# Twelve start offsets inside the split weight tiles of a two-layer hybrid decoder

## The chip, the core and the metric

The kernel runs on one core of a Trainium2 chip. The metric is the device time of one execution in microseconds. The kernel before took 1251.52 us, the median of 2 runs that lie between 1251.26 and 1251.78 us.

## What is computed

Two decoder layers over 512 tokens of width 1024, all in float32. Cut to its skeleton:

```python
def hybrid_layer(x, p_i, positions, ...):
    h = x @ w_in                                  # 1024 -> 1704 columns: queries, keys, values, indexer
    oa = swa_sink_attention(...)                  # 8 heads, window of 128, learned sinks
    ob = dsa_sparse_attention(...)                # 8 heads, the 128 best keys of each query
    mix = concatenate([oa, ob]) @ w_o             # 1024 x 1024
    x = layer_norm(DN_ALPHA * x + mix)
    g, u = split(x @ w_gu, 2)                     # 1024 -> 2 x 2816
    ffn = (silu(g) * u) @ w_down                  # 2816 -> 1024
    ple = (p_i @ w_pp) * sigmoid(x @ w_pg)        # 256 x 1024 and 1024 x 1024
    return layer_norm(DN_ALPHA * x + ffn + ple)

def reference(x, ...):
    x = layer_norm(x)
    for i in range(2):
        x = hybrid_layer(x, ...)
    return x
```

## The kernel before, in words

Every large product is made of three TensorE matmuls. A float32 operand is kept as two parts, a rounded one ("high") and what the rounding left ("low"), and `mm3` (lines 323 to 327) adds high x high (L325), high x low (L326) and low x high (L327) into one PSUM bank. In the input projection, the output projection and the second FFN product, the weights are the moving operand of the matmul and 128 tokens the stationary one. In `gate_up` (the first FFN product, lines 862 to 900) the weights are the stationary operand, 128 columns at a time, and the tokens in `fh` and `fl` move. The profile writes an operand list as "bank<-moving,stationary".

**The way of a weight.** A list `wq` names all pieces of weight in the order of their use. `w_dma` loads a piece into a staging tile `wst` (three buffers of 128 x 1024) by a DMA on SP's queue (L240). `w_split` (L246 to L281) makes the two parts of it in a tile `wsp` of 128 x 2 x 1024 elements, of which the pool has five buffers: ScalarE copies the high part (L278), then GpSimd subtracts it from the piece to get the low part (L279). The matmuls read both parts from that tile. `w_take` hands a split piece to the code that multiplies, and `w_rel`, called when the last matmul on it has been written down, lets `w_pump` load and split the next. Of the 218 tiles that pass through the five buffers, 148 are made from staged pieces.

**The second FFN product.** For five of the six groups of columns the product with `w_down` is done by a scheme of seven products on sums and differences of quarters. For it `w_dma` brings eight raw quarters of `w_down` by DMA into eight buffers of another pool, `slots` (L232, 128 x 512 each), `w_sums` and L263 form differences of them on VectorE (L290 to L292), and the branch at L250 splits quarters and differences into `wsp` tiles, 128 x 512 at a time (ScalarE L256, GpSimd L257). These are the other 70 tiles.

**The pool of slots.** `slots` has 28 buffers of 128 x 512 elements, 2 KiB in each partition, given out in turn. They hold the raw quarters, the two parts of the FFN's hidden activations (`factors`, L908), keys and queries of the attention, and the split gate weights of the last part of a layer (L270). Whoever writes a slot first waits until the last user of its former content is done. For the raw quarters that is the DMA on SP's queue, and what stands behind it on that queue waits too.

**Addresses.** Every `wsp` tile begins at a multiple of 512 bytes in its partition, and so do the operands that the matmuls read from it, with one exception: the pieces of 296 columns at the start of a layer stand as rows of 296 elements (1184 bytes) behind each other, three or two in a tile.

The order of the instructions on each engine is fixed when the program is built. Row for row it is the same in the changed kernel on every engine; line numbers apart, only places of memory and some waits for slots differ.

Of the kernel before, what the change touches and what calls it, by code (L numbers as in the profile page):

```python
# [11 lines left out]
F32R = mybir.dt.float32r  # L12
# [20 lines left out]
TAKEN = -3e38  # L33
THETA = 10000.0
QA, KA, QB, KB, QI, NIN = 0, 512, 768, 1280, 1408, 1704
NSLOT, NTMP = 28, 12
D_GI, D_KI, D_K, D_Q, AHEAD = 9.0, 13.0, 8.0, 10.0, 2
IDX_PACE, NSTART, R_MAIN, R_TOP = 1.5, 2, 0.75, 0.001
LAG, FILL = dict(a=1, b=2), {2: 6, 5: -2}
# [57 lines left out]
def hybrid_kernel(ctx: ExitStack, tc: tile.TileContext, x, p, positions, ln_in_g, ln_in_b, w_in,  # L97
# [7 lines left out]
    wsp = ctx.enter_context(tc.tile_pool(name="wsp", bufs=5))  # L105
# [13 lines left out]
    def slot(dt=F32R):  # L119
        return slots.tile([128, 512], dt, name="slot", tag="slot")  # L120
# [53 lines left out]
    def plan(a, *cols, extra=False):  # L174

        wq.append((a, cols, extra))

    def rows(w, k, a, c0, c1):
        return w[k * 128:(k + a) * 128, c0:c1]
# [8 lines left out]
    for l in range(L):  # L188
# [21 lines left out]
        for h in range(2):  # L210
            for k in range(0, KT, 2):
                plan(2, rows(w_pg[l], k, 2, h * 512, (h + 1) * 512), extra=h == 1)
            plan(2, rows(w_pp[l], 0, 2, h * 512, (h + 1) * 512), extra=h == 1)

    wst_live, w_live = {}, {}
    W_AHEAD, ST_AHEAD = 5, 3
    X_AT = {1: 1, 3: 2, 4: 3}
    wpos = dict(dma=0, split=0, use=0, room=W_AHEAD)

    quarter = {}  # L220

# [24 lines left out]
    def w_split(i):  # L246

        if wq[i][0] == "raw":
            return
        if wq[i][0] == "op":  # L250
            src = quarter[wq[i][1]]
            wpos["room"] -= 1
            w = wsp.tile([128, 2, 1024], F32R, name="wsp", tag="wsp")
            w = w.rearrange("p s (a n) -> p s a n", a=2)
            for j in range(2):
                A.copy(w[:, 0, j], src[j])  # L256
                G.tensor_tensor(w[:, 1, j], src[j], w[:, 0, j], OP.subtract)  # L257
            if wq[i][1] == "11":
                quarter["t4"] = src
            if wq[i][1] == "t1":  # L260
                with tc.issue_after(quarter["after"]):
                    for t4, b, t2 in zip(quarter["t4"], quarter["21"], quarter["t2"]):
                        V.tensor_tensor(t4, b, t2, OP.subtract)  # L263
            w_live[i] = [[w[:, r, j] for j in range(2)] for r in range(2)]
            return
        a, cols, extra = wq[i]
        n = sum(ap.shape[1] for ap in cols)
        st = wst_live.pop(i)
        if extra:
            w = [[slot()[:, :n] for _ in range(a)] for _ in range(2)]  # L270
            for k in range(a):
                A.copy(w[0][k], st[:, k * n:(k + 1) * n])
                V.tensor_tensor(w[1][k], st[:, k * n:(k + 1) * n], w[0][k], OP.subtract)  # L273
            w_live[i] = w
        else:
            wpos["room"] -= 1
            w = wsp.tile([128, 2, 1024], F32R, name="wsp", tag="wsp")
            A.copy(w[:, 0, :a * n], st[:, :a * n])  # L278
            G.tensor_tensor(w[:, 1, :a * n], st[:, :a * n], w[:, 0, :a * n], OP.subtract)  # L279
            w = w[:, :, :a * n].rearrange("p s (a n) -> p s a n", a=a)  # L280
            w_live[i] = [[w[:, r, k] for k in range(a)] for r in range(2)]  # L281
# [13 lines left out]
    def w_pump():  # L295
        while True:
            go = False
            staged = sum(e[0] != "op" for e in wq[wpos["split"]:wpos["dma"]])
            if wpos["dma"] < len(wq) and staged < ST_AHEAD:
                w_dma(wpos["dma"])  # L300
                wpos["dma"] += 1
                go = True
            i = wpos["split"]
            if i < wpos["dma"] and (wpos["room"] or wq[i][0] == "raw" or wq[i][2] is True and wq[i][0] != "op"):
                w_split(i)
                wpos["split"] += 1
                go = True
            if not go:
                return

    def w_take():
        i = wpos["use"]
        if wq[i][0] == "raw":
            i += 1
        wpos["use"] = i + 1
        assert i in w_live, (i, wpos)
        return w_live.pop(i)
# [230 lines left out]
    for l in range(L):  # L548
# [416 lines left out]
        for gi, fs in enumerate(GROUPS):  # L965
# [27 lines left out]
            for h in range(2):  # L993
                ps = [acc() for _ in range(NT)]
                n = len(hs)
                for j in range(n):
                    if j % 2 == 0:
                        w = w_take()
# [10 lines left out]
        for b in TAIL:  # L1009
            for h in range(2):  # L1010
# [6 lines left out]
                for k in range(KT):  # L1017
                    w = ws[k // 2]
# [4 lines left out]
                for k in range(2):  # L1023
                    w = ws[4]
# [43 lines left out]
```

## Time and profile before

| | before |
|---|---|
| median of 2 runs | 1251.52 us |
| the profiled execution's own time | 1251.81 us |
| its span, first to last instruction | 1249.7 us |
| mean granted TensorE clock | 0.998 |
| TensorE busy | 1225.9 us, 98% |
| VectorE busy | 765.2 us, 61% |
| GpSimd busy | 682.9 us, 55% |
| ScalarE busy | 576.4 us, 46% |

How to read it: the span is the stretch from the first to the last instruction; what lies around it is 1251.81 - 1249.7 = 2.1 us. Busy time of TensorE counts each matmul from its start to its modelled end, and matmuls overlap, so it says that TensorE nearly always has one in flight, and not at what rate they follow each other. The rate is read from the starts of neighbours in the timeline. A view of waits lists for each engine how long it stood idle before an instruction and which engine's instruction ended that; SPq is SP's queue, which issues the DMAs.

### The profile page before, as it was taken

The numbers are of one execution on the slowest core, as the hardware profiler recorded it, in microseconds if no ns is written. First come the engines' busy times: TensorE is split into PE (matmuls) and PEld (weight loads), VectorE is DVE, ScalarE is ACT, GpSimd is POOL, SyncE is SP. The second block draws the span as 40 slices with busy tenths as digits, with TensorE's granted clock in tenths as the row PEclk, the third lists the DMA queues.
The fourth block names the chain that finished last, engine by engine and source line by source line (L and its number), as shares of the span: only waits on it lengthen the run. The fifth ranks groups of instructions, "written<-read, shape, count | busy, mean of one in ns | idle before, by whom it ended". The sixth has DMA issues, their size and how long they took to land.

```text
span 1249.7 us, 18006 instructions
## 1 busy us (share of the span) xinstructions
PE 1225.9 (98%) x6552; PEld 1029.9 (82%) x6552; DVE 765.2 (61%) x1678; ACT 576.4 (46%) x1193; POOL 682.9 (55%) x555
## 2 busy tenths in 40 slices
PE   7999999999999999999999999999999999999996
PEld 5998777988888888888899987689888888888885
DVE  7699954682727272726677998286555555555365
ACT  6577763442434343433337787534343333333331
POOL 6885532566566666663169754234757575757400
PEclk9999999999999999999999999999999999999999
DMA  5232311333232323034033203114323333321321
GB/s 177 78 92 85 95 42 35 119 118 118 85 118 84 118 85 118 18 118 140 2 89 114 101 21 117 52 54 149 99 87 105 97 105 99 103 83 52 101 84 50
DMA packets 89264, 112.74 MB, mean 90 GB/s; under 512 B 5460, under 2 KB 66132, under 8 KB 89176
## 3 DMA queue, kind: packets, MB, share of 16 engines
q1 hardware_dynamic: 88504, 111.58, 28.5%
q8 instruction: 51, 0.84, 0.3%
q14 instruction: 37, 0.30, 0.1%
q10 hardware_dynamic: 672, 0.03, 0.0%
HBM read 109.49 MB, written 2.10 MB: 89 GB/s over the span
## 4 chain that ended last, share of the span: by engine, by line
PE 82%; POOL 5%; DVE 3%; issue 3%; ACT 3%; DMA 3%; SPq 0%; DVEq 0%; ACTq 0%; POOLq 0%
PE bank L325 24%; PE bank L326 24%; PE bank L327 24%; PE bank L715 3%; PE bank L684 3%; PE bank L721 2%; POOL wsp L279 2%; DMA wst<-in_w_pg_dram 2%; POOL wsp L257 1%; PE bank L523 1%; PE bank L438 1%; PE bank L732 1%; ACT wsp L278 1%; DVE slot L273 1%; POOL slot L517 1%
## 5 line engine op out<-in xcount | busy, mean ns | idle before, releaser
L279 POOL TENSOR_TENSOR wsp<-wst,wsp 128x1024 fp32r<-128x1024 f32 (+2 forms) x148 | 351.3, 2389 | 244.4 <-ACT wsp L278 240.8
L326 PE MATMUL bank<-fl,wsp 128*128 128x512 f32 (+1 forms) x768 | 284.8, 372 | 0.4 <-DVE fl L441 0.4
L325 PE MATMUL bank<-fh,wsp 128*128 128x512 f32 (+1 forms) x768 | 283.6, 372 | 1.0 <-ACT fh L440 1.0
L327 PE MATMUL bank<-fh,wsp 128*128 128x512 f32 (+1 forms) x768 | 283.1, 371 | 0.0
L278 ACT CAST wsp<-wst 128x1024 fp32r<-128x1024 f32 (+2 forms) x148 | 151.6, 1033 | 166.4 <-PE bank L327 126.2
L325 PE MATMUL bank<-wsp,fh 128*128 128x256 f32 (+3 forms) x512 | 165.2, 326 | 3.6 <-DVE work L648 2.0
L874 DVE TENSOR_TENSOR t2k<-bank,t2k 128x512 f32<-128x512 f32 x44 | 30.4, 692 | 222.0 <-PE bank L327 222.0
L326 PEld LDWEIGHTS bank<-fl,wsp 128*128 128x128 f32 x768 | 144.6, 188 | 25.7 <-DVE fl L441 0.9
L325 PEld LDWEIGHTS bank<-fh,wsp 128*128 128x128 f32 x768 | 143.6, 188 | 26.8 <-ACT fh L440 1.9
L327 PEld LDWEIGHTS bank<-fh,wsp 128*128 128x128 f32 x768 | 144.6, 188 | 24.9
L327 PE MATMUL bank<-wsp,fl 128*128 128x256 f32 (+3 forms) x512 | 163.7, 322 | 1.4 <-DVE fl L441 0.8
L326 PE MATMUL bank<-wsp,fh 128*128 128x256 f32 (+3 forms) x512 | 164.7, 322 | 0.0
L257 POOL TENSOR_TENSOR wsp<-slot,wsp 128x512 fp32r<-128x512 f32 x100 | 141.6, 1442 | 29.0 <-ACT wsp L256 29.0
L325 PE MATMUL bank<-wsp,slot 128*128 128x512 f32 x392 | 153.8, 392 | 0.0
L326 PE MATMUL bank<-wsp,slot 128*128 128x512 f32 x392 | 152.7, 390 | 0.0
L327 PE MATMUL bank<-wsp,slot 128*128 128x512 f32 x392 | 148.4, 390 | 0.0
L790 DVE TENSOR_TENSOR x<-bank,x 128x512 f32<-128x512 f32 x140 | 91.5, 684 | 88.5 <-PE bank L327 88.5
L904 ACT CAST slot<-t2k 128x256 fp32r<-128x256 f32 (+1 forms) x104 | 49.8, 497 | 144.1 <-DVE t2k L874 102.5
L257 POOL TENSOR_TENSOR wsp<-t2k,wsp 128x512 fp32r<-128x512 f32 x40 | 57.5, 1448 | 92.4 <-ACT wsp L256 92.4
L325 PEld LDWEIGHTS bank<-wsp,fh 128*128 128x128 f32 x512 | 97.6, 191 | 11.9 <-ACT fh L440 2.4
L327 PEld LDWEIGHTS bank<-wsp,fl 128*128 128x128 f32 x512 | 97.5, 191 | 7.9 <-DVE fl L441 1.1
L326 PEld LDWEIGHTS bank<-wsp,fh 128*128 128x128 f32 x512 | 98.0, 191 | 6.5 <-issue 1.2
(152 smaller groups left out, 2004.6 us busy)
## 6 DMA issues: line engine op xcount, KB each, us to landing
wst<-in_w_gu_dram SPq DMA_DIRECT2D x88, 512.0 KB, 3.5
slot<-in_w_down_dram SPq DMA_DIRECT2D x80, 256.0 KB, 2.8
wst<-in_w_in_dram SPq DMA_DIRECT2D x16, 512.0 KB, 3.6
wst<-in_w_o_dram SPq DMA_DIRECT2D x16, 512.0 KB, 3.8
wst<-in_w_pg_dram SPq DMA_DIRECT2D x16, 512.0 KB, 4.2
wst<-in_w_in_dram SPq DMA_DIRECT2D x8, 256.0 KB, 2.7
lng<-in_ln_g_dram SPq DMA_DIRECT2D x4, 512.0 KB, 4.8
lnb<-in_ln_b_dram SPq DMA_DIRECT2D x4, 512.0 KB, 5.5
```

What stands on the lines that cost most here:

```text
L257: G.tensor_tensor(w[:, 1, j], src[j], w[:, 0, j], OP.subtract)
L278: A.copy(w[:, 0, :a * n], st[:, :a * n])
L279: G.tensor_tensor(w[:, 1, :a * n], st[:, :a * n], w[:, 0, :a * n], OP.subtract)
L325: PE.matmul(o, sh, mh, start=start, stop=False, skip_group_check=again)
L326: PE.matmul(o, sh, ml, start=False, stop=False, skip_group_check=again)
L327: PE.matmul(o, sl, mh, start=False, stop=stop, skip_group_check=again)
L684: PE.matmul(ps[:, o:o + nn], qT[kind, t, g][:, j * 128:(j + 1) * 128], kT[c, s][:, k0:k0 + nn], start=(s == 0), stop=(s == 1))
L715: PE.matmul(o[u * 64:(u + 1) * 64], vt[b0 + b][:, c * 64:(c + 1) * 64], pts[b][:, u], start=b == 0, stop=b == nb - 1)
L721: PE.transpose(ps[:, j * 128:(j + 1) * 128], es[j][:, b * 128:(b + 1) * 128], idf)
L790: V.tensor_tensor(xt[t][:, c], ps, xt[t][:, c], OP.add)
L874: V.tensor_tensor(a, ps[1, f], a, OP.mult)
L904: A.copy(h[0], src)
```

## The change

A tile `wsp` gets 2176 instead of 2 x 1024 elements in each partition: 128 elements, 512 bytes, of room. The content, 2048 elements, no longer begins at the tile's start. The first tile's content begins at element 0, the second's at element 1, then 2, 4, 8, 12, 16, 24, 32, 48, 64 and 96, and from the thirteenth on the twelve offsets come in turn again. In bytes they are 0, 4, 8, 16, 32, 48, 64, 96, 128, 192, 256 and 384. All five buffers still begin at multiples of 512 bytes. Of the 218 tiles 37 begin at 4 or 8 bytes, 36 at 16 or 48 bytes, and the others at multiples of 32.

The five larger buffers take 5 x 512 bytes more in each partition, and the pool `slots` has 26 buffers in the place of 28, which frees 2 x 2048 bytes. No instruction is added, removed or moved.

```diff
-NSLOT, NTMP = 28, 12
+NSLOT, NTMP = 26, 12
...
+    AT = (0, 1, 2, 4, 8, 12, 16, 24, 32, 48, 64, 96)
+
+    def split_pair():
+
+        w = wsp.tile([128, 2176], F32R, name="wsp", tag="wsp")
+        at = AT[wpos["taken"] % len(AT)]
+        wpos["taken"] += 1
+        return w[:, at:at + 2048].rearrange("p (s n) -> p s n", s=2)
+
...
-    wpos = dict(dma=0, split=0, use=0, room=W_AHEAD)
+    wpos = dict(dma=0, split=0, use=0, room=W_AHEAD, taken=0)
...
             src = quarter[wq[i][1]]
             wpos["room"] -= 1
-            w = wsp.tile([128, 2, 1024], F32R, name="wsp", tag="wsp")
+            w = split_pair()
             w = w.rearrange("p s (a n) -> p s a n", a=2)
...
             wpos["room"] -= 1
-            w = wsp.tile([128, 2, 1024], F32R, name="wsp", tag="wsp")
+            w = split_pair()
             A.copy(w[:, 0, :a * n], st[:, :a * n])
             G.tensor_tensor(w[:, 1, :a * n], st[:, :a * n], w[:, 0, :a * n], OP.subtract)
```

## The prediction

> **What bounds the kernel now.** I read the page first: its busy times and the chain that ended last.
>
> ```profile
> PE 1225.9 (98%) x6552; PEld 1029.9 (82%) x6552; DVE 765.2 (61%) x1678; ACT 576.4 (46%) x1193; POOL 682.9 (55%) x555
> ...
> PE 82%; POOL 5%; DVE 3%; issue 3%; ACT 3%; DMA 3%; SPq 0%; DVEq 0%; ACTq 0%; POOLq 0%
> PE bank L325 24%; PE bank L326 24%; PE bank L327 24%; PE bank L715 3%; PE bank L684 3%; PE bank L721 2%; POOL wsp L279 2%; DMA wst<-in_w_pg_dram 2%; POOL wsp L257 1%; PE bank L523 1%; PE bank L438 1%; PE bank L732 1%; ACT wsp L278 1%; DVE slot L273 1%; POOL slot L517 1%
> ```
>
> 72% of the chain are the three matmuls of `mm3`, and those read the tiles that the change moves. GpSimd's two lines that fill them hold 3% together. Next I asked whom TensorE waits for. These are all rows of that view:
>
> ```profile
> PE bank L345 <- DMA t2k<-in_ln_in_b_dram: 3.0, 1, 3.0
> PE bank L438 <- DVE x L400: 2.0, 1, 2.0
> PE bank L325 <- DVE work L648: 2.0, 2, 1.0
> PE bank L325 <- ACT fh L440: 1.9, 8, 0.2
> PE bank L684 <- ACT slot L524: 1.4, 2, 0.8
> PE bank L327 <- DVE fl L441: 0.8, 1, 0.8
> PE bank L327 <- DVE lns L358: 0.6, 1, 0.6
> PE bank L325 <- ACT slot L613: 0.6, 1, 0.6
> PE bank L523 <- POOL slot L517: 0.5, 2, 0.3
> PE bank L326 <- DVE fl L441: 0.4, 2, 0.2
> PE bank L715 <- ACT t2k L723: 0.2, 1, 0.2
> PE bank L326 <- DVE slot L273: 0.2, 1, 0.2
> ```
>
> They make 13.6 us of 1249.7, and no row has a `wsp` tile as its releaser: no matmul stood waiting for a split weight. So the kernel ends when TensorE has streamed its matmuls, and what counts is their rate. In a stretch of the first FFN product, from start to start:
>
> ```profile
> 289.72 0.39 PE L325 MATMUL bank<-fh,wsp 128*128 128x512 f32 x1
> ...
> 291.99 0.39 PE L326 MATMUL bank<-fl,wsp 128*128 128x512 f32 x1
> ```
>
> Ten starts lie between these, so one matmul of 512 columns takes (291.99 - 289.72) / 10 = 0.227 us. The 0.39 of the row is the time from its start to its modelled end, which overlaps the next.
>
> **The change part by part.** No instruction is added or removed, and none changes its place on its engine. Four things can change: the rate at which matmuls stream a shifted tile as moving operand, the loads of shifted weights as stationary operand, the time of the copies that fill the tile, and the waits for slots.
>
> *Moving operand.* By the counts of the three lines, 3 x (512 + 392) = 2712 matmuls move a `wsp` tile and 3 x 768 = 2304 have it stationary:
>
> ```profile
> L326 PE MATMUL bank<-fl,wsp 128*128 128x512 f32 (+1 forms) x768 | 284.8, 372 | 0.4 <-DVE fl L441 0.4
> L326 PE MATMUL bank<-wsp,fh 128*128 128x256 f32 (+3 forms) x512 | 164.7, 322 | 0.0
> L326 PE MATMUL bank<-wsp,slot 128*128 128x512 f32 x392 | 152.7, 390 | 0.0
> ```
>
> The trace of before shows one place where such a read begins elsewhere than at a multiple of 512 bytes: the pieces of 296 columns, whose rows begin at 0, 1184 and 2368 bytes, that is 0, 160 and 320 bytes behind such a multiple. `project` takes row after row, three matmuls each; the first of each three:
>
> ```profile
> 633.30 0.29 PE L325 MATMUL bank<-wsp,fh 128*128 128x296 f32 x1
> ...
> 633.71 0.30 PE L325 MATMUL bank<-wsp,fh 128*128 128x296 f32 x1
> ...
> 634.11 0.30 PE L325 MATMUL bank<-wsp,fh 128*128 128x296 f32 x1
> ...
> 634.52 0.30 PE L325 MATMUL bank<-wsp,fh 128*128 128x296 f32 x1
> ...
> 634.93 0.30 PE L325 MATMUL bank<-wsp,fh 128*128 128x296 f32 x1
> ```
>
> The steps are 0.41, 0.40, 0.41 and 0.41 us, over all three starts. So a start at 160 or 320 bytes costs nothing that shows, and 160 is no multiple of 64. That covers the offsets that are multiples of 32 bytes: 145 of the 218 tiles. For the other 73 (4, 8, 16 and 48 bytes) no row exists. Their lower bound is the same zero. For the upper I take one more step of 32 bytes, 8 columns, for each read. The price of a column comes from the same lines at 256 columns:
>
> ```profile
> 225.36 0.28 PE L327 MATMUL bank<-fh,wsp 128*128 128x256 f32 x1
> 225.36 0.19 PEld L326 LDWEIGHTS bank<-fl,wsp 128*128 128x128 f32 x1
> ...
> 226.43 0.28 PE L325 MATMUL bank<-fh,wsp 128*128 128x256 f32 x1
> ```
>
> Nine steps in 1.07 us are 0.119 us each; (227 - 119) / 256 = 0.42 ns a column. Eight columns are 3.4 ns, and 2712 x 73/218 = 908 matmuls make 3.1 us. I take zero, since the nearest row, the 296 columns, shows zero. The Trainium skill, "SBUF — State Buffer", section "Specifications (TRN2)", speaks against that: it says that memory is read in lines of 16 bytes, each new line costing something. By it a read of 512 columns that begins at 4 or 8 bytes touches 129 lines for 128, an estimate of 1.7 ns for each of some 460 matmuls, and the sum would be 0.8 us higher. No run so far shows a start inside such a line.
>
> *Stationary operand.* The rows at 225.36 show a weight load of 0.19 us beside matmuls that follow each other at 0.119 us, so loads keep up with that pace too. Where the matmuls have 512 columns they come every 0.227 us, and a load could come 0.108 us later without being the limit. Only the matmuls of 256 columns, 3 x 128 of these 2304, have no such cover. Zero.
>
> *The copies.* GpSimd and ScalarE write and read the same tiles.
>
> ```profile
> L279 POOL TENSOR_TENSOR wsp<-wst,wsp 128x1024 fp32r<-128x1024 f32 x134 | 323.6, 2430 | 202.3 <-ACT wsp L278 198.7 <-DMA wst<-in_w_pg_dram 2.7
> 440.00:503.00 63.00, 63.00 (x279) 52.17 (x278) 32.43 (x46) 23.69 (x38) 39.42 (x23) 1.00 0.32 101
> ```
>
> The last row is one FFN group: GpSimd (the fifth busy time) works 39.4 of 63 us, ScalarE 23.7, while TensorE is full. A tenth more in both stays under that cover. Where the cover is gone is the end of each layer, where the chain goes through a split and then the DMA that waits for its staging tile:
>
> ```profile
> 554.47 2.39 POOL wsp L279
> ...
> 562.63 2.40 POOL wsp L279
> 565.35 2.40 POOL wsp L279
> 567.77 3.82 DMA wst<-in_w_pg_dram
> ```
>
> Five or six such splits a layer lie there. If the 73 tiles' copies took a fifth longer, that is 11 x 2.4 x 0.2 x 73/218 = 1.8 us in the whole. If on the other hand they went 5% faster for all tiles, the chain's share of GpSimd's two lines (3% of 1249.7, 37 us) would give back 1.9 us. I take zero between them, since the offsets of 32 bytes and more leave whole steps as they were.
>
> *Two slots less.* The eight raw quarters of a group wait for slots already:
>
> ```profile
> 440.39 26.19 SPq L232 DMA_DIRECT2D slot<-in_w_down_dram  x8
> 474.47 28.38 SPq L240 DMA_DIRECT2D wst<-in_w_gu_dram  x8
> 501.67 1.14 ACT L256 CAST wsp<-slot 128x512 fp32r<-128x512 f32 x2 [1.68 <-PE bank L327]
> 450.96 3.43 POOL L257 TENSOR_TENSOR wsp<-slot,wsp 128x512 fp32r<-128x512 f32 x2
> 467.01 3.81 POOL L257 TENSOR_TENSOR wsp<-slot,wsp 128x512 fp32r<-128x512 f32 x3 [2.72 <-ACT wsp L256]
> ```
>
> With 26 buffers each takes over the slot that was given out two later. For the second load (issued at 440.9) that is one which the POOL copies of 450.96 read until 454.4, 13.5 us later; for the eighth it is one that the second of the three copies from 467.01 releases at 469.6, 3.4 us after its 466.2. Behind them on SP's queue the next weight load goes at 474.47, still 4.9 us later, held as now by its own staging tile. The first reader of a raw quarter starts at 501.67, over 30 us after the eighth has gone, and a load lands within 6.4 us at most:
>
> ```profile
> DMA to landing us min/median/max: 2.6/2.8/6.4
> ```
>
> So the delay is hidden by 25 us or more, and nothing queued behind moves. Zero; for the eighth load the cover is gone at a delay of 501.67 - 466.2 - 6.4 = 29 us.
>
> *The sum* is made against the profiled execution: span 1249.7 and 2.1 us around it, 1251.8 us, which is 0.3 us above the median 1251.5 of the runs shown. 0 + 0 + 0 + 0 leaves 1251.5 us. Its own range goes from -1.9 (copies) to +3.1 + 1.8, with 0.5 us for runs: 1249 to 1257 us.
>
> **The rivals.** *Slower: the matmul's read of a shifted tile is halved.* If a start that is no multiple of 16 bytes makes each read fetch two pieces in the place of one, every moving read of the 37 tiles at 4 and 8 bytes doubles. The mean width of these matmuls is some 415 columns, 174 ns by the price above, and 2712 x 37/218 = 460 of them make 80 us, all on TensorE's path: 1332 us. It decides from 54 ns a matmul on (25 us). For it speaks that no row of before has such a start; against it, that 160 bytes, which also begins inside a block of 64, costs nothing.
>
> *Faster: part of a matmul's time is a clash that the common start makes.* 512 columns at 0.42 ns are 216 ns; 11 ns of the 227 don't go with the width. If they came from the moving and the stationary read beginning at the same place modulo 512 bytes, eleven of twelve offsets would take them away: 5016 x 11/12 x 11 ns = 51 us, 1201 us. The Trainium skill, "TensorE: Matmul & The Clock Gate", section "Back-to-back issue gap", gives 2.5 ns for that fixed part; by it an estimate of 8 to 9 ns a matmul is open to be won, 40 us. Against the rival stand the rows of 296 columns: their moving reads begin 160 and 320 bytes off the stationary ones, which stand at multiples of 512, and their pace doesn't differ from that at 0.
>
> *Slower, but little: the copies of the 37 tiles take twice as long.* The chain holds 37 us of GpSimd's two lines; 37 x 37/218 = 6.3 us longer, and about as much again that is just hidden now, chiefly at the start of a layer: 1258 to 1264 us. The same row of 63 us against it: in steady groups the two or three odd tiles of a group cost 6 us of GpSimd's 23 idle ones.
>
> **How the numbers follow.** The forecast gets 0.88, the doubled copies 0.03, the halved read 0.06, the clash 0.03. A measurement of this kernel tells about 2% (25 us) from no change: the first two are within it, 0.91; slower by more 0.06; faster by more 0.03. The predicted time is that of the likeliest, 1251.5 us. The range of 8 in 10 takes its bounds and a part of the doubled copies: 1248 to 1259 us.
>
> **What would show it.** Right: matmuls of 512 columns at 0.227 us whatever the tile, TensorE's waits still without a `wsp` releaser, the last raw quarter of a group issued some 3 us later and nothing else moved. Wrong: single triples of 512 columns over 0.70 us, always on tiles at 4 or 8 bytes (halved read), or a pace of 0.216 us (clash), or L279 with two levels of duration and rows "wsp L279" among TensorE's waits (copies).

## The result and the profile after

The changed kernel takes 1268.51 us, the median of 2 runs between 1268.35 and 1268.66, against 1251.52 us before: a ratio of 1.0136 with a 95% interval of 1.0092 to 1.0179, 17.0 us slower. The profiled execution took 1268.35 us with a span of 1266.6 us, 16.9 us more than the span before, at the same granted clock of 0.998.

The page of the changed kernel, busy times and chain. All its line numbers behind the new function are 9 higher, so L334 to L336 are the three matmuls of `mm3`, L287 and L288 the copies from staging:

```profile
PE 1242.5 (98%) x6552; PEld 1029.7 (81%) x6552; DVE 760.4 (60%) x1678; ACT 576.4 (46%) x1193; POOL 666.5 (53%) x555
...
PE 89%; POOL 3%; ACT 2%; DVE 2%; issue 2%; DMA 2%; SPq 0%; DVEq 0%; POOLq 0%; ACTq 0%
PE bank L334 26%; PE bank L335 26%; PE bank L336 26%; PE bank L724 3%; PE bank L693 3%; PE bank L730 2%; POOL wsp L288 1%; DMA wst<-in_w_in_dram 1%; PE bank L532 1%; DMA wst<-in_w_pg_dram 1%; PE bank L447 1%; PE bank L741 1%; POOL slot L526 1%; PE bank L654 0%; POOL t2k L522 0%
```

ScalarE is busy for the same 576.4 us as before, GpSimd for 16 us less, TensorE for 17 us more. The three matmuls now hold 78% of the chain instead of 72%. TensorE's waits, of which these are three of twelve rows:

```profile
PE bank L354 <- DMA t2k<-in_ln_in_b_dram: 3.1, 1, 3.1
PE bank L334 <- ACT fh L449: 2.4, 9, 0.6
...
PE bank L693 <- ACT slot L533: 1.4, 2, 0.8
```

The twelve make 13.7 us, against 13.6 before, and still none of them waits for a `wsp` tile. So nothing feeds TensorE later; it is slower by itself. The timeline of the first FFN product shows where. First the tile whose content begins at 256 bytes (each row gives the start and the time to the modelled end), then one at 64 bytes; its last row is the first matmul on the next tile:

```profile
385.60 0.39 PE L334 MATMUL bank<-fh,wsp 128*128 128x512 f32 x1
...
387.64 0.39 PE L334 MATMUL bank<-fh,wsp 128*128 128x512 f32 x1
```

```profile
264.14 0.39 PE L334 MATMUL bank<-fh,wsp 128*128 128x512 f32 x1
264.37 0.40 PE L335 MATMUL bank<-fl,wsp 128*128 128x512 f32 x1
264.60 0.39 PE L336 MATMUL bank<-fh,wsp 128*128 128x512 f32 x1
264.83 0.40 PE L334 MATMUL bank<-fh,wsp 128*128 128x512 f32 x1
265.07 0.39 PE L335 MATMUL bank<-fl,wsp 128*128 128x512 f32 x1
...
266.94 0.40 PE L334 MATMUL bank<-fh,wsp 128*128 128x512 f32 x1
```

Nine steps in 2.04 us are 0.227 us each, the pace of before. Twelve steps in 2.80 us are 0.233 us each. In nanoseconds the steps at 64 bytes soon alternate: 231, 236, 231, 236 and so on. Nothing waits there and the weight loads take what they took before:

```profile
L335 PEld LDWEIGHTS bank<-fl,wsp 128*128 128x128 f32 x768 | 144.5, 188 | 28.8 <-DVE fl L450 0.9
```

For all matmuls that read a `wsp` tile I took the steps from start to start out of both traces. The mean leaves out steps over 1.25 times the median (waits and changes of stage); the sum leaves out none:

| columns, role of the tile | matmuls | before: mean ns, sum us | after: mean ns, sum us |
|---|---|---|---|
| 512, stationary | 1920 | 226.7, 435.5 | 232.1, 445.7 |
| 512, moving | 1560 | 227.2, 357.6 | 232.2, 365.4 |
| 384, moving | 192 | 174.4, 33.8 | 174.6, 33.8 |
| 296, moving | 192 | 136.3, 31.5 | 138.0, 30.7 |
| 256, moving | 768 | 119.6, 95.0 | 119.4, 94.9 |
| 256, stationary | 384 | 119.7, 47.5 | 118.1, 46.9 |

The two rows of 512 columns are 10.2 + 7.8 = 18.0 us longer and the others 1.5 us shorter, together 16.5 of the 16.9 us by which the span grew. Tiles at every offset but 0 and 256 bytes pay, at 4 as at 384 bytes: between neighbours on the same tile, the 512-column steps with the tile stationary take 228.5 ns at 0 and 227.7 at 256 bytes, and 230.4 to 234.2 at the ten other offsets; with the tile moving 229.3 and 230.0, and 231.3 to 237.0. Matmuls that read no `wsp` tile are as before.

### The profile page after: what moved, and what is told of

Same layout as the page of the kernel before. It is cut to its first block, busy times and chain, and to the rows that moved or that the text cites. A ratio compares the mean times of both kernels' runs of the same rounds, so it can differ in the third digit from the quotient of the medians.

```text
span 1266.6 us, 17996 instructions
## 1 busy us (share of the span) xinstructions
PE 1242.5 (98%) x6552; PEld 1029.7 (81%) x6552; DVE 760.4 (60%) x1678; ACT 576.4 (46%) x1193; POOL 666.5 (53%) x555
## 4 chain that ended last, share of the span: by engine, by line
PE 89%; POOL 3%; ACT 2%; DVE 2%; issue 2%; DMA 2%; SPq 0%; DVEq 0%; POOLq 0%; ACTq 0%
PE bank L334 26%; PE bank L335 26%; PE bank L336 26%; PE bank L724 3%; PE bank L693 3%; PE bank L730 2%; POOL wsp L288 1%; DMA wst<-in_w_in_dram 1%; PE bank L532 1%; DMA wst<-in_w_pg_dram 1%; PE bank L447 1%; PE bank L741 1%; POOL slot L526 1%; PE bank L654 0%; POOL t2k L522 0%
## 5 line engine op out<-in xcount | busy, mean ns | idle before, releaser
L288 POOL TENSOR_TENSOR wsp<-wst,wsp 128x1024 fp32r<-128x1024 f32 (+2 forms) x148 | 341.4, 2321 | 263.1 <-ACT wsp L287 262.8
L335 PE MATMUL bank<-fl,wsp 128*128 128x512 f32 (+1 forms) x768 | 287.8, 375 | 0.4 <-DVE fl L450 0.4
L334 PE MATMUL bank<-fh,wsp 128*128 128x512 f32 (+1 forms) x768 | 287.0, 377 | 1.0 <-ACT fh L449 1.0
L336 PE MATMUL bank<-fh,wsp 128*128 128x512 f32 (+1 forms) x768 | 286.1, 375 | 0.0
L287 ACT CAST wsp<-wst 128x1024 fp32r<-128x1024 f32 (+2 forms) x148 | 151.4, 1032 | 170.7 <-PE bank L336 141.6
L334 PE MATMUL bank<-wsp,fh 128*128 128x256 f32 (+3 forms) x512 | 165.3, 326 | 4.0 <-DVE work L657 1.9
L336 PEld LDWEIGHTS bank<-fh,wsp 128*128 128x128 f32 x768 | 144.8, 189 | 28.4
L334 PEld LDWEIGHTS bank<-fh,wsp 128*128 128x128 f32 x768 | 143.5, 188 | 29.3 <-ACT fh L449 1.9
L336 PE MATMUL bank<-wsp,fl 128*128 128x256 f32 (+3 forms) x512 | 163.6, 322 | 1.3 <-DVE fl L450 0.8
L334 PE MATMUL bank<-wsp,slot 128*128 128x512 f32 x392 | 155.9, 398 | 0.0
L335 PE MATMUL bank<-wsp,slot 128*128 128x512 f32 x392 | 154.6, 394 | 0.0
L266 POOL TENSOR_TENSOR wsp<-slot,wsp 128x512 fp32r<-128x512 f32 x100 | 135.4, 1380 | 33.1 <-ACT wsp L265 33.0
L336 PE MATMUL bank<-wsp,slot 128*128 128x512 f32 x392 | 150.4, 395 | 0.0
L334 PEld LDWEIGHTS bank<-wsp,fh 128*128 128x128 f32 x512 | 96.9, 190 | 12.7 <-ACT fh L449 2.8
L336 PEld LDWEIGHTS bank<-wsp,fl 128*128 128x128 f32 x512 | 96.8, 190 | 8.4 <-DVE fl L450 1.1
```

The source lines that it names most:

```text
L334: PE.matmul(o, sh, mh, start=start, stop=False, skip_group_check=again)
L335: PE.matmul(o, sh, ml, start=False, stop=False, skip_group_check=again)
L336: PE.matmul(o, sl, mh, start=False, stop=stop, skip_group_check=again)
```

## The experiments

Theory A, formed on these rows: the pace of a matmul of 512 columns depends on how its moving read and the stationary read lie to each other, modulo 256 bytes. Rivals: B, each read that doesn't begin at a multiple of 256 bytes is slower by itself; C, the two slots less or the new places of the pools; D, it is the change of the offset from tile to tile; E, starts off a multiple of 16 or 64 bytes; F, the copies' writes to a shifted tile. Beside each time stands the time of the kernel before on the same chip. Of the kernels I show the same row, TensorE between 320 and 400 us, nearly all of it matmuls of 512 columns: length, busy time, the matmuls in it (those that the edges cut are counted too), granted clock and DMA. The kernel before and the changed one:

```profile
320.00:400.00 80.00, 80.00 (x355) 1.00 0.27 86
```

```profile
320.00:400.00 80.00, 80.00 (x347) 1.00 0.28 86
```

**Room and slots alone.**

```diff
-    AT = (0, 1, 2, 4, 8, 12, 16, 24, 32, 48, 64, 96)
+    AT = (0,)
```

> The change with its room of 512 bytes and its 26 slots, but every tile's content at offset 0. Theory A (the matmul's pace depends on how its moving read and the stationary read lie to each other modulo 256 bytes): all operands are again at multiples of 256 bytes, so matmuls of 512 columns come every 227 ns and the time is that of before, 1251.5 us within 2 us. Theory C (the two slots less, or the new places of the pools, cost the time): 1268 us.

1251.29 us beside 1252.10, ratio 0.9992 (0.9982 to 1.0002).

```profile
320.00:400.00 80.00, 80.00 (x354) 1.00 0.29 86
```

C falls. The whole price belongs to the offsets. This run also shows the slots, at the pace of before, on SP's queue:

```profile
453.14 17.13 SPq L241 DMA_DIRECT2D slot<-in_w_down_dram  x8
474.82 28.39 SPq L249 DMA_DIRECT2D wst<-in_w_gu_dram  x8
```

The eight raw quarters begin 12.7 us later than before and end at 470.27, 3.7 us later; the weight load behind them starts at 474.82 instead of 474.47, the 0.35 us by which this execution runs behind the other there (0.36 us for the first reader of a raw quarter, 502.03 against 501.67).

**One offset for all.**

```diff
-    AT = (0, 1, 2, 4, 8, 12, 16, 24, 32, 48, 64, 96)
+    AT = (16,)
```

> As the change, but every tile's content at 64 bytes instead of twelve offsets in turn. Theory A, and theory B (a read that doesn't begin at a multiple of 256 bytes is itself slower), both: about 233 ns where the weights are stationary and 231 where they move, so 1920 x 6 ns + 1560 x 4 ns = 18 us more than before, 1270 us. Theory D (it is the change of the offset from tile to tile that costs): 1251.5 us, since no offset changes.

1265.97 us beside 1252.10, ratio 1.0109 (1.0094 to 1.0125): 13.9 us slower.

```profile
320.00:400.00 80.00, 80.00 (x346) 1.00 0.28 86
```

D falls as the cause: no offset changes, and the matmuls are nearly as slow as with twelve offsets. Stationary reads of 512 columns take 233.3 ns (+12.7 us), moving ones 230.7 (+5.4 us). What the forecast of 1270 us missed is that the narrow matmuls became faster: 256 columns take 117.1 ns moving and 116.3 stationary, 1.8 + 1.3 us less than before.

**Everything shifted.** This is an edit of the kernel before, not of the changed one.

```diff
-NSLOT, NTMP = 28, 12
+NSLOT, NTMP = 26, 12
...
+    pad = const.tile([128, 16], F32, name="pad")
+    G.memset(pad, 0.0)
     fh = const.tile([128, KT, S], F32R, name="fh")
```

> The kernel before with 26 slots and a pad of 64 bytes ahead of all tiles: weights, tokens and slots all begin 64 bytes behind a multiple of 256, so none is shifted against another. Theory A (only the place of the two reads to each other counts): 227 ns and 1251.5 us within 2 us. Theory B (each read off a multiple of 256 bytes costs by itself): at least the 1270 us of the run with 64 bytes for the weights alone.

1252.05 us beside 1252.10, ratio 0.9998 (0.9989 to 1.0008).

```profile
320.00:400.00 80.00, 80.00 (x354) 1.00 0.27 86
```

Weights, tokens and slots all begin 64 bytes behind a multiple of 256, and every row of the table is back at its value of before (226.7 and 227.2 ns for 512 columns). B falls: a start off the boundary costs nothing as long as the partner is off by the same.

**Multiples of 256 bytes.**

```diff
-    AT = (0, 1, 2, 4, 8, 12, 16, 24, 32, 48, 64, 96)
+    AT = (0, 64)
```

> As the change, but the offsets are 0 and 256 bytes in turn. Theory A with a period of 256 bytes: 227 ns and 1251.5 us within 2 us. If the period were 512 bytes, half of the tiles would be out of step: 8 to 9 us more, 1260 us. Theory D (a changing offset costs): about 1268 us.

1251.42 us beside 1252.10, ratio 0.9996 (0.9987 to 1.0006).

```profile
320.00:400.00 80.00, 80.00 (x354) 1.00 0.28 86
```

The period is 256 bytes or divides them, and a changing offset is free when it is a multiple of that.

**All starts within 256 bytes.** The pieces of weight get a kind: "q" for the query columns of the input projection, "g" for the first pieces of the first FFN product, both read 256 columns wide, "w" for the rest.

```diff
+        k = kind.get(i, "w")
+        n = seen[k] = seen.get(k, -1) + 1
+        at = {"w": n * 27 % 64, "q": n * 4 % 64, "g": n * 4 + 4}[k]
```

> A look at the price by offset, with the same 26 slots: the tiles read 512 columns wide go through all 64 starts of 4 bytes inside 256, the tiles read 256 columns wide through sixteen starts in steps of 16 bytes (moving) and eight (stationary). Theory A: matmuls of 512 columns at 226 to 228 ns only where both reads start at the same place modulo 256 bytes, 229 to 238 ns elsewhere, no start below 226; about 1268 us in all. If the price came from starts that are no multiples of 16 or 64 bytes (theory E), the starts at 64, 128 and 192 bytes would be as cheap as 0.

A single run: 1267.79 us beside 1251.94. Steps of matmuls of 512 columns whose neighbours read the same tile, by the start's remainder modulo 16 bytes, without the start at 0:

| start modulo 16 bytes | 0 | 4 | 8 | 12 |
|---|---|---|---|---|
| tile moving, mean ns | 233.0 | 236.1 | 234.0 | 229.9 |
| tile stationary, mean ns | 232.4 | 233.3 | 232.0 | 231.2 |

E falls: 64, 128 and 192 bytes cost 233.3, 233.1 and 231.0 ns stationary and 230.0, 232.8 and 233.4 moving, while the start at 0 shows 228.4 and 230.8 here. Only the moving one at 64 bytes, with eight steps, is no dearer than the start at 0 in this run; the run with 64 bytes for all has it at 230.7 against 227.2. For a moving tile, starts 12 bytes into a block of 16 are the cheapest and starts 4 bytes into it the dearest, which no theory had said. The expectation missed in two points. Stationary tiles at 252 and at 120 bytes reach 226.7 and 227.0 ns, so the same place isn't the only good one. And the start at 0 is itself above 227 ns here: after a tile with another offset the pace takes several matmuls to come back, as 229, 232, 231 and then 227 ns after one such change in the changed kernel. So D has a small share. No start had a mean below 226.7 ns.

**The narrow tiles alone.** The kinds "q" and "g" as in the scan; all other tiles stand at 0.

```diff
+    AT = {'q': 16, 'g': 16}
...
+        at = AT.get(kind.get(i), 0)
```

> Only the tiles whose matmuls are 256 columns wide stand at 64 bytes (the query columns of the input projection and the first pieces of the first FFN product), all others at 0. From the run with 64 bytes everywhere: 768 moving reads at 117.1 for 119.6 ns and 384 stationary at 116.3 for 119.7 ns, 1.9 + 1.3 = 3.2 us less than before, 0.3% faster. If the gain of the narrow ones belonged to the whole mix and not to their own offset: the time of before.

1249.00 us beside 1251.94, ratio 0.9977 (0.9968 to 0.9986): 0.23% or 2.9 us faster, for 3.2 us expected. In this kernel, first pieces of the first FFN product:

```profile
224.31 0.28 PE L338 MATMUL bank<-fl,wsp 128*128 128x256 f32 x1
...
226.46 0.28 PE L339 MATMUL bank<-fh,wsp 128*128 128x256 f32 x1
```

Nineteen steps in 2.15 us are 0.113 us each, where before nine took 1.07 us, 0.119 each. The matmuls of 512 columns kept their pace:

```profile
320.00:400.00 80.00, 80.00 (x355) 1.00 0.29 89
```

**Only stationary tiles of 512 columns shifted.** Against the kernel with the narrow tiles shifted:

```diff
-                        if f == 0:
+                        if f > 0:
                             kind[len(wq)] = "g"
...
-    AT = {'q': 16, 'g': 16}
+    AT = {'g': 16}
```

> Only the tiles that are stationary for 512 columns (the first FFN product but for its first pieces) stand at 64 bytes, all others at 0. Theory A: only these 1920 matmuls go from 226.7 to 233.3 ns, 12.7 us more than before, 1264 us; the 1560 moving reads of 512 columns stay at 227.2 ns. If a shifted tile disturbed its neighbours too (theory D): the moving ones slower as well, up to 1270 us.

1264.74 us beside 1251.94, ratio 1.0104 (1.0088 to 1.0120): 12.8 us slower for 12.7 expected.

```profile
320.00:400.00 80.00, 80.00 (x347) 1.00 0.28 86
```

The stationary ones are at 233.4 ns, the moving ones at 227.5.

**Their partner shifted too.** The kernel just told, and:

```diff
+    pads = [const.tile([128, 16], F32, name="pad0")]
     fh = const.tile([128, KT, S], F32R, name="fh")
     fl = const.tile([128, KT, S], F32R, name="fl")
+    pads.append(const.tile([128, 48], F32, name="pad1"))
+    for pad in pads:
+        G.memset(pad, 0.0)
```

> The run with 64 bytes for the wide tiles of the first FFN product, and the tokens (fh and fl), which are their partner in the matmul, moved by 64 bytes too. Theory A: these 1920 matmuls come back to 226.7 ns although tile, copies and slots stand as in that run. Now 384 + 192 other matmuls of 512 columns are out of step (6 ns each, +3.4 us), and 768 + 384 narrow ones are too (-2 to -3.5 ns each, -3.3 us): 1251 to 1253 us. Theory B, or the copies' writes to a shifted tile as the cause (theory F): these 1920 stay at 233 ns and the time at 1264 us or above.

1252.50 us beside 1251.52, ratio 1.0007 (0.9997 to 1.0016).

```profile
320.00:400.00 80.00, 80.00 (x354) 1.00 0.29 87
```

The 1920 matmuls are back at 227.3 ns. The two pads take 256 bytes together, so tiles, copies and slots keep their places modulo 256 bytes; only the tokens that these tiles meet in TensorE have moved against them. F falls, and B once more; A holds.

**Another place for the narrow ones.** Against the kernel with the narrow tiles at 64 bytes:

```diff
-    AT = {'q': 16, 'g': 16}
+    AT = {'q': 48, 'g': 16}
```

> As the run with 64 bytes for the narrow tiles alone, but the query columns' tiles at 192 bytes. In the run that moved the tokens by 64 bytes these 768 moving reads lay at 192 bytes to their partner and took 115.7 ns; in the run with 64 bytes 117.4. So 768 x 1.7 ns = 1.3 us less than that run's 1249.0 us, 1247.7 us, 0.3% under before.

1248.50 us beside 1251.65, ratio 0.9975 (0.9966 to 0.9984). The moving reads of 256 columns took 116.5 ns, not 115.7, and the span is the same 1246.7 us as at 64 bytes. The intervals of the two overlap nearly whole: faster than before, and not to be told from the version at 64 bytes. The stationary reads of 256 columns, at 64 bytes in both, took 116.8 ns there and 115.2 here, so a nanosecond or two between two such kernels says little about a place.

## Why the prediction was wrong

*What bounds the kernel* was right. TensorE's pace decides, and it is the pace that changed; every other path was as loose as read.

*Two slots less* was right to the point: with this part alone the second load went some 14 us later for 13.5 forecast and the eighth 3.7 us for 3.4, both with 0.35 us of that execution's lag in them; nothing behind them moved, and the kernel with this part alone takes 1251.29 us.

*The copies* cost nothing, as forecast, and no row of TensorE's waits has a `wsp` releaser. But they did not stay as they were. Two rows of the changed kernel's timeline, and all 134 together:

```profile
85.75 2.00 POOL L288 TENSOR_TENSOR wsp<-wst,wsp 128x1024 fp32r<-128x1024 f32 x1 [0.21 <-ACT wsp L287]
...
89.64 2.40 POOL L288 TENSOR_TENSOR wsp<-wst,wsp 128x1024 fp32r<-128x1024 f32 x1
...
L288 POOL TENSOR_TENSOR wsp<-wst,wsp 128x1024 fp32r<-128x1024 f32 x134 | 315.0, 2364 | 220.5 <-ACT wsp L287 220.2
```

The first of these fills a tile at 8 bytes, the second one at 16. The mean of 2364 ns against 2430 hides two levels: the 20 copies into tiles at 4 and 8 bytes have a median of 2.00 us, the others 2.40 as before. The scan shows the same for all its starts: 2.00 us at 4 or 8 bytes behind a multiple of 16, 2.40 at 0 or 12. So the sign "L279 with two levels of duration" came, but the other way round from the rival that it was meant for: the copies into these tiles got a sixth shorter and not twice as long. It is off the path and changed nothing in the time; its cause stays open. ScalarE's L287 took 1052 ns against 1053 before.

*Moving operand* is the step that failed first. "So a start at 160 or 320 bytes costs nothing that shows" holds for the rows under it, matmuls of 296 columns: in nanoseconds they take 136.3 and 136.8 at these starts and 135.7 at 0 in the kernel before. What failed is "That covers the offsets that are multiples of 32 bytes", which carried them over to 512 columns. With 64 bytes for all tiles the width decides: the shift leaves 384 columns within a nanosecond, gives 2.5 to 3.4 ns back at 256 and costs 3.5 (moving) to 6.6 ns (stationary) at 512. The term taken as 0, at most 3.1 us, measured 7.8 us at 512 columns with twelve offsets.

*Stationary operand* failed as well: "a load could come 0.108 us later without being the limit". Loads did not get later or longer, 188 ns as before. The argument asked only whether a load comes in time. It left out that a load runs while another matmul streams its moving operand, as the rows at 225.36 in the prediction show, and that the place of the one read against the other could set the pace of the stream. Its zero measured 10.2 us, the larger half. The narrow ones, which I had singled out as without cover, gained 0.6 us.

*The rivals.* The halved read was wrong in kind: no offset came near 54 ns, the worst mean of the scan was 239 ns. Its sign, triples over 0.70 us, did come, but not on tiles at 4 or 8 bytes alone: in the changed kernel 29 of 56 triples at 4 bytes are over it, and 37 of 84 at 32. The clash was the nearest to the truth and had the wrong sign at 512 columns: the place of the two reads to each other, modulo a power of two, does set the pace, but the common start is among the best and not the clash, and the period is 256 bytes. I held the rows of 296 columns against it, again across the width. The bound of 3.1 us was made for a cost inside one read, so the range could not hold a cost between two. And 2%, taken as what a measurement tells from no change, was too coarse: the interval of 0.92 to 1.79% is clear of zero with two runs of each kernel. The rule on lines of 16 bytes, from the Trainium skill's "SBUF — State Buffer", section "Specifications (TRN2)", gave an estimate of 0.8 us in the prediction. The scan does show a pattern of 16 bytes for moving tiles, but with the price at its highest at 4 bytes and its lowest at 12; counting lines touched gives no such difference, nor the price at 64 or 128 bytes.

*What stays open:* what in the chip ties the pace to the place of the two reads, why the steps fall into regular patterns such as 231 and 236 ns, and why narrow matmuls gain where wide ones lose. Of the 227 ns at 512 columns the 11 ns that don't go with the width are untouched: no start took them away.

## What to carry to other kernels

Where TensorE streams wide matmuls back to back, keep both operands' tiles at the same place modulo 256 bytes; a pad or an odd tile size that moves one operand against the other cost 2% of each such matmul here, with no wait in the profile to show it, and moving the partner by the same amount healed it. Read the pace from start to start of neighbours in the timeline, since the busy share stayed at 98%. A null from one width of matmul is no null for another: take the row of the width that carries the sum.

## What was not expected of the hardware

Shifted pairs are faster at 256 columns: means of 115 to 117 ns in place of 120 with 64 bytes between the two reads (113 in the stretch shown), and a kernel that shifts only these tiles is 0.23% faster than the one before (0.14 to 0.32%). And a tile's offset is felt past its end: after a change the pace takes several matmuls to settle. And GpSimd's subtraction of 128 x 1024 elements takes 2.00 us in place of 2.40 when the tile that it writes and reads begins 4 or 8 bytes behind a multiple of 16.
